# Splitting w_in and w_out once and keeping the parts in DRAM; cache rows moved in 128 and in 16 pieces

## The chip, the core and the metric

The kernel runs on one core of a Trainium2 chip. The metric is the device time of one execution in microseconds (us): the median of three runs. A run is also profiled, and that execution has a time of its own. The core has a matrix engine (TensorE, PE in the profile, with PEld for its weight loads), a vector engine (VectorE, DVE), an activation engine (ScalarE, ACT), a general engine (GpSimd, POOL), and an engine that only issues transfers (SyncE, SP). Each engine works through its own instructions in order, and engines wait for one another and for transfers at semaphores. All transfers of this kernel are issued by SP, one after another.

## The reference, cut to what matters

One layer (DEPTH is 1) works on 2048 prompt rows and 8 sample rows, each of width 1024, all in float32:

```
z = rmsnorm(x) @ w_in                       # 1024 x 1536: q, k, v, conv a and g, ssm u
mix = [attention(q, k, v) | conv(a, g) | ssm(u)]
x = x + mix @ w_out                         # 1024 x 1024
x = x + (silu(hf @ w_gate) * (hf @ w_up)) @ w_down   # hf = rmsnorm(x), 2816 hidden columns
y = rmsnorm(x)
```

Attention has a window of 128 keys. A sample row attends to the 128 rows of its own cache (cache_swa_k and cache_swa_v, each 8 x 128 x 2 x 64). Outputs besides y are the last rows of k, v, conv input and ssm state, and for the samples the caches shifted by one row: rows 1 to 127 of each key and value cache become rows 0 to 126 of the output, and row 127 is the new one. The conv cache (8 x 30 x 256) is shifted in the same way.

## The kernel before

Rows are handled in four quarters of 512 columns (the last has 520, with the 8 samples), transposed so that channels lie on the partitions. A product of float32 matrices is made of three passes of the matrix engine over a high and a low part: weight high by input high, weight high by input low, weight low by input high. So every 128-column block of a weight is first split. `load_unit` does it: SP loads the block (1024 x 128, 512 KB) into a raw tile `wraw` (two buffers), ACT copies it rounded to `whl[:, 0]`, and POOL writes the rest, raw minus rounded, to `whl[:, 1]` (128 x 2 x 1024, 1 MB; three buffers).

Up to the feed-forward part the blocks are used by quarter: twelve blocks of w_in (2 for u, 4 for the conv's g and a, 6 for k, v and q) and then eight of w_out, so each block is loaded and split four times: 48 and 32 units. `w_stream` runs the w_in products; ssm, conv and attention of the quarters run beside it, and their outputs go through DRAM (`mix`). `out_stream` runs the w_out products and `gate_up` and `down` the feed-forward part in two halves, each with its weights loaded anew.

The order of instructions is written by a planner, `Flow`, while the program is built. Tasks say which engine, buffers and events they need next; the planner keeps a clock for each engine, estimates a cost for each instruction (`Engine.cost`), and emits the task that can begin first, with a priority among those close together. The result is a fixed list for each engine, so a changed cost or buffer count moves instructions throughout.

Sample caches are touched at two places. `attn_sample` loads rows 1 to 127 of the key cache into a tile with the row index on the partitions, puts the new row (`nrow`) into the output and into the tile's row 0, and does the same for values. `shift_caches`, at the start of the feed-forward part, copies the shifted rows from the input caches to the outputs inside DRAM.

Of the kernel before, what the change touches and what calls it, by code (L numbers as in the profile page):

```python
# [9 lines left out]
F32 = mybir.dt.float32  # L10
F32R = mybir.dt.float32r
# [150 lines left out]
class Engine:  # L162
# [8 lines left out]
    def cost(self, op, out, ins, args, kw):  # L171
        n = 1
        for d in out.shape[1:]:
            n *= d
        psum = any(x.space == PSUM for x in ins)
        if self.name == "PE":
            if op == "transpose":
                return max(54.0, args[1].shape[0] / 1.2 + 2.5)
            if ins[0].dtype == F32R:
                return max(107.0, n / 2.4 + 2.5)  # L180
            ns = max(215.0, n / 0.6 + 6.0)
            return ns / 2 + 1.0 if out.shape[0] <= 64 else ns
# [29 lines left out]
def hybrid_step(  # L212
# [42 lines left out]
    nsink = const.tile([P, NH], F32, name="nsink")  # L255

    psum = ctx.enter_context(tc.tile_pool(name="psum", bufs=1, space=PSUM))
    wpool = ctx.enter_context(tc.tile_pool(name="wpool", bufs=3))
    hpool = ctx.enter_context(tc.tile_pool(name="hpool", bufs=2))
    stage = ctx.enter_context(tc.tile_pool(name="stage", bufs=1))  # L260
# [5 lines left out]
    spool = segA.enter_context(tc.tile_pool(name="spool", bufs=1))  # L266
    kpool = segA.enter_context(tc.tile_pool(name="kpool", bufs=1))
    N_ST, N_X, N_S2, N_CU = 6, 2, 7, 3
    fl.buffers(mm=3, sc=3, tr=2, wraw=2, whl=3, h=2, stg=N_ST, x=N_X, acc=1, cu=N_CU, s2=N_S2, s4=2, u=2, ssmA=1,
               ssmB=1)  # L270


# [36 lines left out]


    class Unit:
        def __init__(self, load):
            self.load, self.ready, self.hl = load, Ev(), None

    def load_unit(u, prio, pool=None, tag="whl", bufs=3, after=0.0):

        def one():
            yield "SP", "wraw"
            raw = wpool.tile([P, 1024], F32, tag="wraw", name="wraw", bufs=2)
            u.load(raw)  # L320
            yield "ACT", tag
            hl = (pool or wpool).tile([P, 2, 1024], F32R, tag=tag, name=tag, bufs=bufs)
            S.activation(hl[:, 0, :], raw, AF.Copy)
            yield "POOL"
            G.tensor_tensor(hl[:, 1, :], raw, hl[:, 0, :].bitcast(F32), op=OP.subtract)
            rel("wraw")
            u.hl = hl.rearrange("p h (k c) -> p h k c", c=P)
            u.ready.hit(fl.now())
        fl.add(one(), -1e6 + prio, after=after)

    def cols_unit(w, c0s):

        def load(raw):
            r3 = raw.rearrange("p (k c) -> p k c", c=P)
            n = P // len(c0s)
            wv = w.rearrange("(k p) c -> p k c", p=P)
            for i, c0 in enumerate(c0s):
                dma(r3[:, :, i * n:(i + 1) * n], wv[:, :, c0:c0 + n])
        return Unit(load)

    def rows_unit(w, f):
        return Unit(lambda raw: dma(raw, w[f * P:(f + 1) * P, :]))
# [1 line left out]
    def out_unit(m):  # L344


        def load(raw):
            r3 = raw.rearrange("p (k c) -> p k c", c=P)
            cs = slice(m * P, (m + 1) * P)
            for g in range(2):  # L350
                dma(r3[64 * g:64 * g + 64, 0:4, :],
                    w_out[0, 256 * g:256 * g + 256, cs].rearrange("(j p) c -> p j c", p=64))
            dma(r3[:, 4:6, :], w_out[0, 512:768, cs].rearrange("(k p) c -> p k c", p=P))
            for l in range(2):
                dma(r3[:, 6 + l, :], dap(w_out, (768 + 16 * l) * D + m * P, [[32 * D, 8], [D, 16], [1, P]]))
        return Unit(load)

    def product(ps, n, terms, evs=None):

# [99 lines left out]

    def w_units(q, kind):  # L460
        if kind == "u":
            return [("u", i, cols_unit(w_in[0], [1280 + i * P])) for i in range(2)]
        if kind == "c":
            return [(k, i, cols_unit(w_in[0], [b + i * P])) for i in range(2) for k, b in (("g", 1024), ("a", 768))]
        return ([("k", 0, cols_unit(w_in[0], [512])), ("v", 0, cols_unit(w_in[0], [640]))]
                + [("q", j, cols_unit(w_in[0], [64 * j, 256 + 64 * j])) for j in range(4)])

    def w_stream(plan):
        first = []
# [773 lines left out]
    plan = w_plan([(int(x[0]), x[1:]) for x in "0c 0u 1k 0k 1u 1c 2c 2u 3u 2k 3k 3c".split()])  # L1243
    outs = [out_unit(m) for _ in range(4) for m in range(KT)]
    for i, u in enumerate([p[3] for p in plan] + outs):
        load_unit(u, i)
    for q in range(4):
        fl.add(prep_h(q), -2e6 if q == 0 else -1000 + q)
    fl.add(cu_tiles(), -2e6)
# [11 lines left out]
    def s_tile():  # L1261
        return apool.tile([P, 4, 256], F32, tag="s", name="s", bufs=5)
# [175 lines left out]
            mix_ev[q, k].hit(fl.now())  # L1438

    def attn_sample():  # L1440
        yield "SP", kvq_ev[3], dist_ev
        kvT = apool.tile([P, 2, NS], F32, tag="kvT", name="kvT")
        dma(kvT[:, 0, :], kT_d[3][:, 512:520])
        dma(kvT[:, 1, :], vT_d[3][:, 512:520])
# [9 lines left out]
        V.tensor_copy(nrow, pt[:NS, 0:256].rearrange("p (i c) -> p i c", c=P))  # L1454
        rel("tr")
        V.tensor_tensor(qs[:, 0], qs[:, 0], qs[:, 1], op=OP.add)
        yield "SP", "s", "s", "s", "x2"
        kc, vc, kT = [s_tile().rearrange("p j k -> p (j k)").rearrange("p (b c) -> p b c", c=P) for _ in range(3)]
        for i, (t, src, dst) in enumerate(((kc, cache_k, o_ks), (vc, cache_v, o_vs))):
            dma(t[1:P], src[0, :, 1:P].rearrange("b t g d -> t b (g d)"))  # L1460
            dma(dst[0, :, 127].rearrange("b g d -> b (g d)"), nrow[:, i, :])
            dma(t[0:1].rearrange("o b c -> o (b c)").rearrange("o (b c) -> o b c", c=P), nrow[:, i, :])
        for a in range(2):
# [331 lines left out]

    def shift_caches():

        for src, dst in ((cache_k, o_ks), (cache_v, o_vs)):
            yield "SP"
            dma(dst[0, :, 0:127].rearrange("b t g d -> t b (g d)"), src[0, :, 1:128].rearrange("b t g d -> t b (g d)"))  # L1800
        yield "SP"
        dma(o_convs[0, :, 0:29, :].rearrange("b t c -> t b c"), cache_conv[0, :, 1:30, :].rearrange("b t c -> t b c"))

    fl.add(shift_caches(), 300, after=t0)

# [38 lines left out]
    def final(q, i, dst, c0, n):  # L1844
# [26 lines left out]
        if tag == "y":  # L1871
            y = fpool.tile([P, D], F32, tag="y", name="y", bufs=2)
        else:
            y = wpool.tile([P, 2, D], F32R, tag="whl", name="y3").bitcast(F32)[:, 0]
        V.tensor_tensor(st[:n, 0:1], st[:n, 0:1], st[:n, 1:2], op=OP.add)
        yield "ACT"
        S.activation(st[:n, 1:2], st[:n, 0:1], AF.Sqrt, scale=1.0 / D, bias=eps[:n])
# [57 lines left out]
```

## Time and profile before

| | |
|---|---|
| median of three runs | 2398.83 us (2397.98 to 2400.85) |
| the profiled execution | 2399.17 us, span of its instructions 2397.2 us |
| busy: PE, DVE, ACT, POOL | 93%, 49%, 31%, 27% of the span |
| bytes moved | 212.24 MB by the program's queue |

The span is cut below into stretches: 0 to 857 us holds everything ahead of the feed-forward part, 857 to 2397 us the feed-forward part. A row that gives busy time of an engine in a stretch says how much of it the engine worked; the granted clock (PEclk) is 1 for the matrix engine's full speed of 2.4 GHz and 0.5 for 1.2 GHz.

### The profile page before, as it was taken

To read this page: it belongs to the slowest core of one execution; us is meant where nothing else is said; L and a number is where in the kernel's file an instruction comes from. 1 tells how busy PE (TensorE), PEld (TensorE's weight loads), DVE (VectorE), ACT (ScalarE), POOL (GpSimd) and SP (SyncE) were. 2 spreads that over 40 slices of the span, in tenths; PEclk is the share of its full clock that TensorE was granted. 3 is DMA by queue.
4 is the path that set the end of the run, shared out by engine and by line. 5 is a ranking of instruction groups with operands and counts; after the bars stand their busy time and mean duration, and the time that the engine had idled before them with its cause. 6 is when DMAs were issued, how large, how long until landed. Compare 5 with 4: busy or idle time off the path is not lost.

```text
span 2397.2 us, 31412 instructions
## 1 busy us (share of the span) xinstructions
PE 2222.3 (93%) x12518; PEld 1865.2 (78%) x12518; DVE 1163.1 (49%) x2177; ACT 731.6 (31%) x1324; POOL 644.2 (27%) x329
## 2 busy tenths in 40 slices
PE   8878977939899994999999999999999999999998
PEld 8656756737667883888888888888999898989997
DVE  6997979939996551222222222246233332322234
ACT  6227633726665320111111111136111111111113
POOL 3473442212335431221222212221222112222220
PEclk9989988969999997999999999999999999999999
DMA  6444534525646651111111111126111111111101
GB/s 181 114 124 132 132 90 125 152 64 167 181 145 194 195 174 59 53 44 44 53 53 53 40 40 44 53 76 211 53 53 36 45 45 48 45 49 53 53 27 71
DMA packets 301192, 214.24 MB, mean 89 GB/s; under 512 B 61491, under 2 KB 263622, under 8 KB 301046
## 3 DMA queue, kind: packets, MB, share of 16 engines
q1 hardware_dynamic: 301046, 212.24, 30.1%
q8 instruction: 98, 1.61, 0.3%
q14 instruction: 48, 0.39, 0.0%
HBM read 172.39 MB, written 40.48 MB: 89 GB/s over the span
## 4 chain that ended last, share of the span: by engine, by line
PE 74%; DVE 15%; SPq 4%; DMA 2%; POOL 2%; issue 2%; ACT 1%; DVEq 0%; ACTq 0%; POOLq 0%
PE mm L207 47%; PE sc L207 23%; DVE s L207 5%; SPq L149 4%; DVE acc L207 4%; PE tr L207 3%; DVE h L207 1%; POOL s L207 1%; POOL whl L207 1%; DVE stg L207 1%; DVE sst L207 1%; DMA wraw<-in_w_ff_gate 1%; DVE x L207 1%; DVE t L207 1%; DVE ET L207 1%
## 5 line engine op out<-in xcount | busy, mean ns | idle before, releaser
L207 PE MATMUL mm<-h,whl 128*128 128x512 f32 (+2 forms) x7824 | 1508.7, 351 | 24.7 <-DVE stg L207 10.8
L207 PEld LDWEIGHTS mm<-h,whl 128*128 128x128 f32 x7824 | 1256.1, 191 | 234.9 <-issue 12.6
L207 POOL TENSOR_TENSOR whl<-wraw,whl 128x1024 fp32r<-128x1024 f32 x168 | 425.2, 2531 | 1209.3 <-ACT whl L207 1083.1
L207 PE MATMUL sc<-act,whx 128*128 128x512 f32 (+2 forms) x2640 | 507.8, 351 | 29.2 <-ACT act L207 28.9
L207 PEld LDWEIGHTS sc<-act,whx 128*128 128x128 f32 x2640 | 426.9, 189 | 100.2 <-ACT act L207 29.4
L207 DVE TENSOR_TENSOR xa<-xa,sc 128x512 f32<-128x512 f32 (+2 forms) x440 | 255.4, 582 | 340.9 <-PE sc L207 340.8
L207 ACT ACTIVATE whl<-wraw 128x1024 fp32r<-128x1024 f32 x168 | 178.0, 1059 | 640.3 <-PE mm L207 468.5
L207 DVE TENSOR_TENSOR stg<-stg,mm 128x512 f32<-128x512 f32 (+2 forms) x110 | 64.0, 582 | 616.3 <-ACT stg L207 314.5
L207 DVE SCALAR_TENSOR_TENSOR acc<-cu,taps,acc 128x512 f32<-128x512 f32 x240 | 216.6, 964 | 0.0
L207 POOL TENSOR_TENSOR whx<-wraw,whx 128x1024 fp32r<-128x1024 f32 x44 | 105.7, 2402 | 367.1 <-ACT whx L207 352.7
L207 ACT ACTIVATE act<-stg 128x512 fp32r<-128x512 f32 (+2 forms) x110 | 60.2, 548 | 429.5 <-DVE stg L207 429.5
L207 DVE TENSOR_TENSOR act<-stg,act 128x512 fp32r<-128x512 f32 (+2 forms) x110 | 96.6, 878 | 66.7 <-ACT act L207 66.7
L207 ACT ACTIVATE whx<-wraw 128x1024 fp32r<-128x1024 f32 x44 | 46.3, 1052 | 220.2 <-PE sc L207 220.2
L207 ACT ACTIVATE stg<-mm 128x512 f32<-128x512 f32 (+2 forms) x144 | 75.1, 522 | 84.0 <-PE mm L207 83.9
L207 ACT ACTIVATE s<-s,sst 128x256 f32<-128x256 f32 (+1 forms) x184 | 85.2, 487 | 15.7 <-DVE sst L207 15.6
L207 ACT ACT_TABLE_LOAD x59 | 75.7, 1283 | 4.0 <-DMA out<-s 1.7
L207 POOL TENSOR_TENSOR stg<-stg 128x512 f32<-128x512 f32 (+2 forms) x33 | 46.0, 1394 | 41.8 <-ACT stg L207 34.3
L207 PE MATMUL sc<-kk,qq 128*128 128x256 f32 (+1 forms) x304 | 44.8, 292 | 10.3 <-DVE mx L207 9.1
L207 PE MATMUL sc<-ident,s 128*128 128x128 f32 x248 | 39.6, 284 | 14.2 <-DVE s L207 10.9
L207 PEld LDWEIGHTS sc<-kk,qq 128*128 128x128 f32 x304 | 39.4, 195 | 13.9 <-DVE mx L207 7.9
L207 PEld LDWEIGHTS sc<-ident,s 128*128 128x128 f32 x248 | 29.1, 142 | 25.5 <-DVE s L207 14.7
L207 DVE CUSTOM_DVE_ANT_0 s<-sc,ndist 128x256 f32<-128x256 f32 (+1 forms) x128 | 45.6, 408 | 2.7 <-PE sc L207 2.6
(201 smaller groups left out, 1206.1 us busy)
## 6 DMA issues: line engine op xcount, KB each, us to landing
wraw<-in_w_ff_gate SPq DMA_DIRECT2D x44, 512.0 KB
wraw<-in_w_ff_up SPq DMA_DIRECT2D x44, 512.0 KB
wraw<-in_w_ff_down SPq DMA_DIRECT2D x44, 512.0 KB
wraw<-in_w_in SPq DMA_DIRECT2D x32, 512.0 KB
wraw<-in_w_out SPq DMA_DIRECT2D x96, 128.0 KB
wraw<-in_w_in SPq DMA_DIRECT2D x32, 256.0 KB
mix<-stg SPq DMA_DIRECT2D x32, 256.0 KB
xo<-in_x_prompt SPq DMA_DIRECT2D x32, 256.0 KB
```

The lines of the kernel that those rows point to most:

```text
L149: r = self.nc.sync.dma_start(out, in_)
L207: return call(*args, **kw)
```

## The change

Four things change in the program.

1. Each block of w_in and w_out is split at its first use only. Its whole `whl` tile (both parts, 1 MB) is then stored to a DRAM tile `kept`; each of the three later uses loads that tile straight into a `whl` buffer, with no `wraw`, ACT or POOL. Of the 80 units 20 are split and stored and 60 are reloaded. A chain of events (`turn`) keeps the units' buffers in order.
2. `whl` has four buffers in place of three.
3. `attn_sample` loads all 128 rows of each sample cache, ahead of its other loads, and `shift_caches` copies each shifted cache as 16 pieces for each of the 8 samples (1016 or 464 elements each) in place of 127 (or 29) rows for each sample.
4. The planner's cost of a matmul of split operands is n / 2.4 + 18 ns for n columns (before + 2.5), and 123 ns at least (before 107).

```diff
             if ins[0].dtype == F32R:
-                return max(107.0, n / 2.4 + 2.5)
+                return max(123.0, n / 2.4 + 18.0)
...
-    fl.buffers(mm=3, sc=3, tr=2, wraw=2, whl=3, h=2, stg=N_ST, x=N_X, acc=1, cu=N_CU, s2=N_S2, s4=2, u=2, ssmA=1,
+    fl.buffers(mm=3, sc=3, tr=2, wraw=2, whl=WB, h=2, stg=N_ST, x=N_X, acc=1, cu=N_CU, s2=N_S2, s4=2, u=2, ssmA=1,
...
+        mine, taken = turn.get(tag), Ev()
+        turn[tag] = taken
+        order = (mine,) if mine else ()
+
+        def again():
+            yield "SP", tag, kept_ev[u.key], *order
+            taken.hit(0.0)
+            hl = (pool or wpool).tile([P, 2, 1024], F32R, tag=tag, name=tag, bufs=bufs)
+            dma(hl.bitcast(F32), kept[u.key])
+            u.hl = hl.rearrange("p h (k c) -> p h k c", c=P)
+            u.ready.hit(fl.now())
 
         def one():
             yield "SP", "wraw"
             raw = wpool.tile([P, 1024], F32, tag="wraw", name="wraw", bufs=2)
             u.load(raw)
-            yield "ACT", tag
+            yield "ACT", tag, *order
+            taken.hit(0.0)
...
             u.ready.hit(fl.now())
+            if keep:
+                yield "SP"
+                dma(kept[u.key], hl.bitcast(F32))
+                kept_ev[u.key].hit(fl.now())
+        if u.key is not None and u.key in kept:
+            fl.add(again(), -1e6 + prio, after=after)
+            return
+        if keep:
+            kept[u.key] = dram.tile([P, 2, 1024], F32, name="hl_%s%d" % u.key)
+            kept_ev[u.key] = Ev()
         fl.add(one(), -1e6 + prio, after=after)
...
     for i, u in enumerate([p[3] for p in plan] + outs):
-        load_unit(u, i)
+        load_unit(u, i, keep=True)
...
     def attn_sample():
-        yield "SP", kvq_ev[3], dist_ev
+        yield "SP", kvq_ev[3], dist_ev, "s", "s", "s", "x2"
+        kc, vc, kT = [s_tile().rearrange("p j k -> p (j k)").rearrange("p (b c) -> p b c", c=P) for _ in range(3)]
+        for t, src in ((kc, cache_k), (vc, cache_v)):
+            dma(t, src[0].rearrange("b t g d -> t b (g d)"))
...
-        yield "SP", "s", "s", "s", "x2"
-        kc, vc, kT = [s_tile().rearrange("p j k -> p (j k)").rearrange("p (b c) -> p b c", c=P) for _ in range(3)]
-        for i, (t, src, dst) in enumerate(((kc, cache_k, o_ks), (vc, cache_v, o_vs))):
-            dma(t[1:P], src[0, :, 1:P].rearrange("b t g d -> t b (g d)"))
+        yield "SP"
+        for i, (t, dst) in enumerate(((kc, o_ks), (vc, o_vs))):
             dma(dst[0, :, 127].rearrange("b g d -> b (g d)"), nrow[:, i, :])
...
-        for src, dst in ((cache_k, o_ks), (cache_v, o_vs)):
+        for src, dst, row, rows in ((cache_k, o_ks, 128, 128), (cache_v, o_vs, 128, 128), (cache_conv, o_convs, 256, 30)):
             yield "SP"
-            dma(dst[0, :, 0:127].rearrange("b t g d -> t b (g d)"), src[0, :, 1:128].rearrange("b t g d -> t b (g d)"))
-        yield "SP"
-        dma(o_convs[0, :, 0:29, :].rearrange("b t c -> t b c"), cache_conv[0, :, 1:30, :].rearrange("b t c -> t b c"))
+            n = (rows - 1) * row // 16
+            dims = [[n, 16], [rows * row, NS], [1, n]]
+            dma(dap(dst, 0, dims), dap(src, row, dims))
```

SP's list where the sample caches are loaded, before (a row is one instruction, with its line, what it writes and reads, the shape, and a count where it stands several times; `mr` are loads for the next quarter's `out_stream` input, `stg<-vT` the values of a quarter for attention):

```order
L149 DMA mr<-mix_78 128x512 x2
L149 DMA wraw<-in_w_out 64x4x128 x2
L149 DMA wraw<-in_w_out 128x2x128
L149 DMA wraw<-in_w_out 128x1x128 x2
L149 DMA s<-in_cache_swa_k 127x8x128
L149 DMA out<-nrow 8x128
L149 DMA s<-nrow 1x8x128
L149 DMA s<-in_cache_swa_v 127x8x128
L149 DMA out<-nrow 8x128
L149 DMA s<-nrow 1x8x128
L149 DMA mr<-mix_78 128x512
L149 DMA stg<-vT_76 128x512
```

The same place in the changed kernel (`kvT` and `qs` are the sample's own rows, `hl_o` the kept blocks of w_out, `x_82` stores of the first quarter's rows, `xo` loads of x):

```order
L149 DMA wraw<-in_w_ff_gate 128x8x128
L149 DMA s<-in_cache_swa_k 128x8x128
L149 DMA s<-in_cache_swa_v 128x8x128
L149 DMA kvT<-kT_73 128x8
L149 DMA kvT<-vT_77 128x8
L149 DMA qs<-qh_65 128x4x8
L149 DMA qs<-ql_69 128x4x8
L149 DMA x_82<-x_5855 128x512
L149 DMA xo<-in_x_prompt 128x4x128
L149 DMA hl_o_200<-whl 128x2048
L149 DMA wraw<-in_w_ff_up 128x8x128
L149 DMA whl<-hl_o_193 128x2048
```

The two cache loads now stand together with 128 rows each, the stores of the new row come later, and the whole place has moved behind the loads of all eight blocks of w_out (before, behind two); stores of kept blocks and their first reloads stand around it.

SP's list at the start of the feed-forward part, before (`wraw` are its weights, `xa` the rows it adds to, `rs` the row norms):

```order
L149 DMA xa<-x_83 128x512 x5
L149 DMA rs_89<-stg 128x520
L149 DMA out<-in_cache_swa_k 127x8x128
L149 DMA wraw<-in_w_ff_gate 128x8x128
L149 DMA wraw<-in_w_ff_up 128x8x128
L149 DMA out<-in_cache_swa_v 127x8x128
L149 DMA out<-in_cache_conv 29x8x256
L149 DMA wraw<-in_w_ff_gate 128x8x128
L149 DMA wraw<-in_w_ff_up 128x8x128
```

The same place in the changed kernel:

```order
L149 DMA wraw<-in_w_ff_gate 128x8x128
L149 DMA xa<-x_83 128x512 x3
L149 DMA wraw<-in_w_ff_up 128x8x128
L149 DMA xa<-x_83 128x512 x2
L149 DMA out<-in_cache_swa_k 16x8x1016
L149 DMA wraw<-in_w_ff_gate 128x8x128
L149 DMA out<-in_cache_swa_v 16x8x1016
L149 DMA wraw<-in_w_ff_up 128x8x128
L149 DMA out<-in_cache_conv 16x8x464
```

The three copies still stand among the weight loads, in 16 outer pieces now, with one weight load between two of them.

POOL's list from the ssm of the second quarter on (`stg<-s,s` is the last product of a quarter's ssm, two for each quarter, `stg<-acc` and the products behind it the conv's norm), before:

```order
L207 TENSOR_TENSOR stg<-s_2595,s_2372 128x512
L207 TENSOR_TENSOR stg<-s_2614,s_2372 128x512
L207 TENSOR_TENSOR whl<-wraw,whl 128x1024 x5
L207 TENSOR_TENSOR stg<-acc 128x512
L207 TENSOR_TENSOR stg<-stg 128x512
L207 TENSOR_TENSOR whl<-wraw,whl 128x1024
L207 TENSOR_TENSOR stg<-s_3122,s_3039 128x512
L207 TENSOR_TENSOR stg<-s_3142,s_3039 128x512
L207 TENSOR_TENSOR stg<-stg,acc 128x512 x2
L207 TENSOR_TENSOR whl<-wraw,whl 128x1024 x3
L207 TENSOR_TENSOR stg<-s_3486,s_3364 128x512
L207 TENSOR_TENSOR stg<-s_3500,s_3364 128x512
```

And in the changed kernel:

```order
L207 TENSOR_TENSOR stg<-s_2481,s_2286 128x512
L207 TENSOR_TENSOR stg<-s_2494,s_2286 128x512
L207 TENSOR_TENSOR stg<-acc 128x512
L207 TENSOR_TENSOR stg<-stg 128x512
L207 TENSOR_TENSOR stg<-stg,acc 128x512 x2
L207 TENSOR_TENSOR stg<-s_3101,s_3029 128x512
L207 TENSOR_TENSOR stg<-s_3123,s_3029 128x512
L207 TENSOR_TENSOR stg<-s_3424,s_3342 128x512
L207 TENSOR_TENSOR stg<-s_3433,s_3342 128x512
L207 TENSOR_TENSOR stg<-acc 128x512
L207 TENSOR_TENSOR stg<-stg 128x512
L207 TENSOR_TENSOR stg<-stg,acc 128x512 x2
```

The splits `whl<-wraw,whl` no longer stand between the ssm and conv work of the second to the last quarter; the next ones are the eight blocks of w_out.

## Rows read from the trace of the kernel before

**Rows 1.** The page's second part: PE's busy tenths in 40 equal slices.

```profile
PE   8878977939899994999999999999999999999998
```

**Rows 2.** Busy time by stretch: engines, instructions, granted clock, DMA share, GB/s.

```profile
core 0: us, PE busy (x) PEld busy (x) DVE busy (x) ACT busy (x) POOL busy (x), PEclk, DMA share, GB/s
0.00:110.00 110.00, 93.17 (x562) 82.78 (x562) 88.89 (x241) 50.65 (x81) 43.71 (x39) 0.92 0.57 149
110.00:484.00 374.00, 318.05 (x2162) 246.82 (x2162) 331.32 (x599) 190.14 (x342) 155.21 (x88) 0.91 0.46 126
484.00:532.00 48.00, 10.60 (x74) 10.01 (x74) 7.17 (x12) 5.78 (x8) 5.04 (x3) 0.64 0.11 35
532.00:650.00 118.00, 108.15 (x591) 84.23 (x591) 112.14 (x305) 77.47 (x208) 35.89 (x21) 0.94 0.61 171
650.00:857.00 207.00, 195.52 (x1107) 158.98 (x1108) 142.67 (x256) 105.55 (x217) 93.63 (x50) 0.97 0.60 176
960.00:2397.00 1437.00, 1426.60 (x7744) 1227.12 (x7742) 449.39 (x733) 285.85 (x449) 295.87 (x123) 1.00 0.18 56
```

**Rows 3.** Who PE waited for, 480 to 600 and 800 to 960 us: total, times, longest.

```profile
PE tr L207 <- DMA stg<-vT: 21.7, 1, 21.7
PE tr L207 <- DMA s<-nrow: 16.2, 1, 16.2
...
PE sc L207 <- ACT act L207: 28.9, 1, 28.9
```

**Rows 4.** SP's instructions in order of time at the sample caches: start, length.

```profile
481.04 0.44 SPq L149 DMA_DIRECT2D s<-in_cache_swa_k  x1
481.57 22.26 SPq L149 DMA_DIRECT2D out<-nrow  x1
...
505.11 22.81 SPq L149 DMA_DIRECT2D out<-nrow  x1
```

**Rows 5.** SP's instructions in order of time at the shifted copies.

```profile
876.16 25.66 SPq L149 DMA_DIRECT2D wraw<-in_w_ff_gate  x1
...
904.91 24.07 SPq L149 DMA_DIRECT2D out<-in_cache_conv  x1
929.10 7.32 SPq L149 DMA_DIRECT2D wraw<-in_w_ff_gate  x1
```

**Rows 6.** Busy time by stretch, right behind the two stops at the caches.

```profile
507.00:511.00 4.00, 3.26 (x14) 2.89 (x14) 0.69 (x1) 0.00 (x0) 0.00 (x0) 0.50 0.07 22
532.00:538.00 6.00, 5.52 (x26) 5.55 (x27) 5.27 (x24) 5.26 (x13) 2.56 (x2) 0.50 0.94 235
```

**Rows 7.** Groups by line and shape, 0 to 860 us: busy, mean | idle before, releaser.

```profile
L207 DVE SCALAR_TENSOR_TENSOR acc<-cu,taps,acc 128x512 f32<-128x512 f32 x240 | 216.6, 964 | 0.0
L207 DVE TENSOR_SCALAR s<-s,sst 128x256 f32<-128x256 f32 x72 | 37.0, 576 | 0.5
...
L207 POOL TENSOR_TENSOR whl<-wraw,whl 128x1024 fp32r<-128x1024 f32 x83 | 220.1, 2653 | 409.0 <-ACT whl L207 282.8 <-issue 58.2 <-DMA qq<-qh 14.0
...
L207 ACT ACTIVATE whl<-wraw 128x1024 fp32r<-128x1024 f32 x83 | 87.8, 1058 | 189.8 <-PE mm L207 112.6 <-DMA wraw<-in_w_in 51.8 <-issue 20.4
```

**Rows 8.** Single tiles' instructions: duration in ns, minimum, median, maximum, first and last start.

```profile
L207 DVE SCALAR_TENSOR_TENSOR acc<-cu,taps,acc x240: 721/744/2905, 49.5 to 705.4; 128x512 f32<-128x512 f32 x120
...
L207 DVE TENSOR_SCALAR s<-s,sst x72: 340/349/2504, 435.1 to 729.5; 128x256 f32<-128x256 f32 x72
```

**Rows 9.** Instructions in order of time near 422 us: start, length.

```profile
421.81 2.35 POOL L207 TENSOR_TENSOR whl<-wraw,whl 128x1024 fp32r<-128x1024 f32 x1 [16.28 <-ACT whl L207]
421.85 2.33 DVE L207 TENSOR_TENSOR sst<-sst,nsink 128x4 f32<-128x4 f32 x1
```

**Rows 10.** The chain that ended last, 110 to 484 us, by engine and line.

```profile
by line: DVE acc L207 18.9%; PE mm L207 18.5%; DVE s L207 16.3%; PE sc L207 14.5%; PE tr L207 6.3%; POOL whl L207 5.3%; POOL s L207 5.0%; issue 4.1%; DVE stg L207 3.2%; DVE tmp_s L207 1.6%; DVE h L207 1.4%; DVE x L207 1.0%; DVE sst L207 0.9
```

**Rows 11.** Busy time by stretch of the instructions that touch whl alone.

```profile
110.00:484.00 374.00, 208.41 (x1016) 164.71 (x1016) 34.95 (x33) 100.35 (x34) 0.91 0.46 126
```

**Rows 12.** Busy time by stretch, where transfers were densest.

```profile
860.00:880.00 20.00, 20.00 (x87) 16.15 (x87) 15.84 (x14) 8.97 (x13) 7.06 (x3) 1.00 0.98 350
```

More of the change, by code (lines that the diff above doesn't have):

```diff
@@ L257, in hybrid_step @@
     psum = ctx.enter_context(tc.tile_pool(name="psum", bufs=1, space=PSUM))
+    WB = 4
     wpool = ctx.enter_context(tc.tile_pool(name="wpool", bufs=3))
@@ L311, in hybrid_step, with __init__, load_unit @@
     class Unit:
-        def __init__(self, load):
-            self.load, self.ready, self.hl = load, Ev(), None
-    def load_unit(u, prio, pool=None, tag="whl", bufs=3, after=0.0):
+        def __init__(self, load, key=None):
+            self.load, self.ready, self.hl, self.key = load, Ev(), None, key
+    kept, kept_ev, turn = {}, {}, {}
+    def load_unit(u, prio, pool=None, tag="whl", bufs=WB, after=0.0, keep=False):
+        mine, taken = turn.get(tag), Ev()
[8 more added lines that the diff above has]
+            u.ready.hit(fl.now())
         def one():
@@ L328, in one, with cols_unit @@
             u.ready.hit(fl.now())
+            if keep:
[8 more added lines that the diff above has]
+            kept_ev[u.key] = Ev()
         fl.add(one(), -1e6 + prio, after=after)
-    def cols_unit(w, c0s):
+    def cols_unit(w, c0s, key=None):
         def load(raw):
@@ L338, in load @@
                 dma(r3[:, :, i * n:(i + 1) * n], wv[:, :, c0:c0 + n])
-        return Unit(load)
+        return Unit(load, key)
     def rows_unit(w, f):
@@ L355, in load @@
                 dma(r3[:, 6 + l, :], dap(w_out, (768 + 16 * l) * D + m * P, [[32 * D, 8], [D, 16], [1, P]]))
-        return Unit(load)
+        return Unit(load, ("o", m))
     def product(ps, n, terms, evs=None):
@@ L461, in w_units @@
         if kind == "u":
-            return [("u", i, cols_unit(w_in[0], [1280 + i * P])) for i in range(2)]
+            return [("u", i, cols_unit(w_in[0], [1280 + i * P], ("u", i))) for i in range(2)]
         if kind == "c":
-            return [(k, i, cols_unit(w_in[0], [b + i * P])) for i in range(2) for k, b in (("g", 1024), ("a", 768))]
-        return ([("k", 0, cols_unit(w_in[0], [512])), ("v", 0, cols_unit(w_in[0], [640]))]
-                + [("q", j, cols_unit(w_in[0], [64 * j, 256 + 64 * j])) for j in range(4)])
+            return [(k, i, cols_unit(w_in[0], [b + i * P], (k, i))) for i in range(2)
+                    for k, b in (("g", 1024), ("a", 768))]
+        return ([("k", 0, cols_unit(w_in[0], [512], ("k", 0))), ("v", 0, cols_unit(w_in[0], [640], ("v", 0)))]
+                + [("q", j, cols_unit(w_in[0], [64 * j, 256 + 64 * j], ("q", j))) for j in range(4)])
     def w_stream(plan):
@@ L1873, in final @@
         else:
-            y = wpool.tile([P, 2, D], F32R, tag="whl", name="y3").bitcast(F32)[:, 0]
+            y = wpool.tile([P, 2, D], F32R, tag="whl", name="y3", bufs=WB).bitcast(F32)[:, 0]
         V.tensor_tensor(st[:n, 0:1], st[:n, 0:1], st[:n, 1:2], op=OP.add)
```

## The prediction

> **What bounds the kernel now.** I read the page's slices first: PE is busy all the time in the last six tenths and has gaps in the first four [rows 1]. The table by stretch says the same in us [rows 2]: from 960 us on PE works 1426.6 of 1437 us at full clock, so nothing that frees another engine or a buffer can be felt there. Ahead of 857 us it works 93.2, 318.1, 10.6, 108.2 and 195.5 us in five stretches, 725 of 857: 132 us stand idle. In the second stretch DVE is the busier engine (331 of 374 us). The third, 484 to 532 us, is different in kind: PE, DVE, ACT and POOL all rest, and the transfers too (share 0.11, against 0.46 and 0.61 on either side).
>
> The waits name who ended the rests: 16.2 and 21.7 us until transfers, and 28.9 us at the start of the feed-forward part behind ACT [rows 3], at a time when the weight loads were held on SP [rows 5]. SP's own rows show why. The load of the key cache is issued in 0.44 us, and then SP's next instruction, a store of 4 KB, is held 22.26 us; behind the value cache the same, 22.81 us [rows 4]. That load is 127 rows x 8 x 512 bytes = 520 KB; over 22.3 us this is 23 GB/s, one sixteenth of the 350 GB/s that all engines reach in the densest stretch [rows 12]. So one transfer engine of 16 carries the whole load, and SP, which works in order, stands behind it with every other transfer. The shifted copies do it again: the weight load behind the first copy is held 25.66 us, the conv copy behind the second 24.07, the next weight load 7.32 [rows 5]. Two places, then, and beside them a DVE bound up to 484 us.
>
> **The change part by part. Cache rows in 128 and 16 pieces.** Rows that divide by 16 should use all engines: 0.52 MB at 350 GB/s is 1.5 us, the two loads and three copies together some 7 us of transfer beside 421 us that are free ahead of 857 us (worked out below). Removed are the rests: 16.2 + 21.7 + 28.9 = 66.8 us. The matmuls right behind the first two ran at a granted clock of 0.5 (1.2 GHz): 3.26 and 5.52 us of work [rows 6], half of it lost time, 4.4 us. **Term 1: -71.2 us.** What is late next? In the stop DVE did 7.2 of 48 us and ACT 5.8 [rows 2], so no engine caught up on work that it would now owe; I keep the whole term. Its other end is nothing, if the new shapes stay on one engine (rival D).
>
> **Splits removed.** Sixty of 80 units lose an ACT copy (1.06 us) and a POOL subtraction (2.65 us) [rows 7]. Neither engine is a bound, but POOL's split stretches DVE's work: at 421.81 us POOL begins a split of 2.35 us, and a DVE operation on four columns that begins 0.04 us later takes 2.33 us and ends with it [rows 9]. How much that is in all I take from mean against median: the conv's 240 multiply-adds have a mean of 964 and a median of 744 ns, 52.8 us over; the softmax's 72 scalings 576 and 349, 16.3 us [rows 7, 8]. Of these 69 us, 60 of 83 splits should give back 50. (Smaller groups would add, other POOL work takes away; I let them cancel.) Only what lies on the path counts: in 110 to 484 us the chain gives DVE 18.9 + 16.3 + 3.2 + 1.6 + 1.4 + 1.0 + 0.9 = 43.3% [rows 10], 162 of its 331 busy us, so 0.49 of it: 24.5 us. The chain also has POOL's splits at 5.3%, 20 us; 34 splits stand in this stretch [rows 11], the last of the first twelve blocks among them, which remain, so I take half, 10. **Term 2: -34.5 us.** Ends: nothing, if PE takes over as the bound at once; and 77 us, all the rest that PE has in 110 to 484, 532 to 650 and 650 to 857 us (55.9 + 9.9 + 11.5).
>
> The Trainium skill has a rule that makes more of it (page "SBUF — State Buffer", section "Who interferes with whom"): a DVE instruction with two SBUF inputs and a GpSimd instruction that reads SBUF exclude each other, and the second to issue waits for the whole of the first. The trace agrees in kind [rows 9]; by the rule at its fullest the 60 splits would hold DVE for their whole length, and the sum would be that of rival B below.
>
> **Stores and reloads.** A kept unit moves 1.05 MB, 3.0 us of all engines at 350 GB/s [rows 12]. A raw block is 0.52 MB; in the feed-forward part, where little but such blocks moves, 56 GB/s take a share of 0.18, so 311 GB/s when full, 1.7 us [rows 2]. Before: 80 x 1.7 = 136 us. After: 20 x (1.7 + 3.0) + 60 x 3.0 = 274. So 138 us more. Free ahead of 857 us, by the shares of its five stretches [rows 2]: 47 + 202 + 43 + 46 + 83 = 421 us. It fits on average. It is tight at the start: twelve stores, 36 us, into 47 free. I let a quarter of that delay first loads. **Term 3: +8 us** (ends 0 and 138).
>
> SP's queue: a store waits for its POOL split, and behind it stands the raw load after next, which waited for the same split before, since that frees its `wraw`: no cost. A reload waits on SP for PE to let go of a buffer; ACT had that wait before, 112.6 us of it [rows 7]. Behind it on SP stand stores of k, q, u and mix, and reads of the next stage. With four buffers three blocks are ahead; 24 matmuls at 208.4 us / 1016 [rows 11] are 4.9 us, so 15 us of cover for a transfer of 3. I cost it at nothing; with the cover gone it is rival C. Where w_out took five issues a block, it takes one now: SP gains, and nobody waits for that.
>
> **Planner numbers and the fourth buffer.** PE's and DVE's work is the same but for a few copies that change places with ACT. The feed-forward part has PE full, so the deeper buffer gives nothing there. The new order can shift waits either way; I cost it at 0 with 10 us on both sides, half of the 21 us for which PE rests in 532 to 857 us.
>
> **Sum.** -71.2 - 34.5 + 8 = -97.7 us on the profiled execution's 2399.2 (span 2397.2 and 2.0 around it): 2301.5. The median of the runs is 0.3 below the profiled one: 2301 us.
>
> **Rivals.**
> A, only the stops go: DVE's stretched operations lie where PE is the bound anyway. For it: PE has 318 of 374 us of work in the DVE stretch, and its work at half clock is not won back by anything. Against: the chain's 43% DVE. 2399.2 - 71.2 + 8 = 2336 us.
> B, every removed split frees DVE for its whole length: 60 x 2.65 x 0.49 = 78 us on the path, capped by PE's 77 us of rest. For it: single operations do stretch by a whole split [rows 9]. Against: half of the operations keep their median [rows 8], so most meet no split. 2399.2 - 71.2 - 77 + 8 = 2259 us. (This is what the page on SBUF would make of it at its fullest.)
> C, slower: the reloads are not hidden, the 138 us of transfers stand on the path of the w_in and w_out products. For it: shares of 0.6 from 532 us on, and SP in order. Against: 421 us free and 15 us of cover. 2399.2 - 71.2 - 34.5 + 138 = 2431 us; it turns slower once more than 106 of the 138 us are felt, 1.8 us for each reload.
> D, the change doesn't do what it says: the new shapes still run on one engine, and the stops stay. 2399.2 - 34.5 + 8 = 2373 us. For it: nothing but that the 8 samples lie inside. By the Trainium skill (page "DMA: Bandwidth & Descriptors", section on why a DMA increments its semaphore by 16) the count of engines is the largest number up to 16 that divides the outermost size, so 1 for 127 and 16 for 128 or 16; the trace agrees for 127 [rows 4].
>
> **How the numbers follow.** Chances: the forecast 0.54 (its own range 2280 to 2322, by the planner's 10 us and about a third of term 2), A 0.24, B 0.13, C 0.05, D 0.04. The range from 2258 to 2340 takes in the forecast, nearly all of A and over half of B, and leaves out C, D and the far side of B. What a measurement can tell is 0.2%, 5 us. A, B, D and the forecast are all faster, C is slower but for a sliver: faster 0.94, same 0.01, slower 0.05.
>
> **What would show it.** Term 1: no SP instruction of 20 us at the caches, no PE wait over 10 us there or at the start of the feed-forward part, and no stretch with every engine at rest. Term 2: a mean of the conv's multiply-adds near 800 ns, fewer than 30 splits ahead of the feed-forward part, DVE's share of the chain there smaller than PE's. Term 3: a share of transfers near 0.7 with reloads landing before PE asks; waits of PE for reloads, or waits of SP for PE that hold mix or u stores, would be C. The feed-forward part should take as long as before less 29 us. Most likely to make me wrong is the size of term 2: it rests on a chain's share, and which engine bounds the first half once the splits are gone is not in this trace.

## The result, and the profile of the changed kernel

The changed kernel takes 2319.07 us in the median (2313.35 to 2322.32), beside 2399.72 for the kernel before, run with it: a ratio of 0.9662, 95% interval 0.9640 to 0.9684, or 80.7 us less. The forecast was 2301 with a range of 2258 to 2340. The profiled execution took 2316.92 us.

The page's first two parts, busy time of the engines and PE's slices (against [rows 1]):

```profile
PE 2213.1 (96%) x12518; PEld 1860.5 (80%) x12518; DVE 1074.2 (46%) x2187; ACT 674.2 (29%) x1261; POOL 473.3 (20%) x263
...
PE   8689989999699999999999999999999999999997
```

The slices of 3 and 4 at the two stops are gone. What stands below 8 now is a 6 in the second slice, a 6 in the eleventh, from 579 us on, and a 7 at the end. DVE is busy for 1074.2 us (before 1163.1), POOL for 473.3 (before 644.2).

Busy time by stretch (columns as in [rows 2]; here the feed-forward part begins at some 806 us):

```profile
0.00:110.00 110.00, 86.86 (x535) 77.26 (x536) 82.74 (x255) 49.23 (x79) 44.39 (x49) 0.91 0.86 263
110.00:484.00 374.00, 340.64 (x2316) 264.79 (x2315) 312.64 (x723) 189.42 (x418) 44.25 (x37) 0.94 0.61 188
484.00:650.00 166.00, 142.26 (x800) 110.42 (x800) 113.59 (x330) 82.78 (x213) 32.77 (x20) 0.92 0.71 215
650.00:810.00 160.00, 152.05 (x866) 129.06 (x865) 91.24 (x120) 51.92 (x87) 44.44 (x29) 0.99 0.74 252
...
880.00:2315.00 1435.00, 1421.27 (x7709) 1222.70 (x7707) 444.49 (x730) 284.80 (x446) 287.88 (x120) 1.00 0.18 55
```

The stretch to 110 us has PE less busy than before (86.9 us against 93.2) with transfers at a share of 0.86, where it was 0.57. From 110 to 484 us PE works 340.6 us (318.1 before). The feed-forward part is full, as it was.

Who PE waited for, 0 to 880 us (total, times, longest; against [rows 3]):

```profile
PE mm L207 <- POOL whl L207: 14.7, 2, 13.6
PE tr L207 <- POOL s L207: 12.9, 1, 12.9
PE sc L207 <- DVE s L207: 12.3, 13, 2.8
PE tr L207 <- POOL stg L207: 11.1, 4, 5.2
...
PE tr L207 <- DMA stg<-in_cache_conv: 5.1, 1, 5.1
PE tr L207 <- ACT ss L207: 4.2, 1, 4.2
```

No wait of 16 to 29 us is left, and none for the key and value caches; one of 5.1 us is for the samples' conv cache. Two of 13 us remain. In the first, at some 83 us, among the stores of the first twelve blocks, PE waits for a split, and POOL's rows show what held it (start, length, and in brackets the idle time before and what ended it):

```profile
91.22 2.46 POOL L207 TENSOR_TENSOR s<-s,PW 128x128 f32<-128x128 f32 x3 [16.94 <-DVE s L207]
93.64 2.78 POOL L207 TENSOR_TENSOR whl<-wraw,whl 128x1024 fp32r<-128x1024 f32 x1
```

ACT had rounded the block by 87.4 us. In POOL's order the split stands behind a product of the ssm's set-up, for which POOL waited 16.9 us until DVE was done.

SP's instructions at the sample caches and at the shifted copies, in order of time (start, length; against [rows 4, 5]):

```profile
580.84 0.79 SPq L149 DMA_DIRECT2D s<-in_cache_swa_k  x1
581.73 2.94 SPq L149 DMA_DIRECT2D s<-in_cache_swa_v  x1
...
592.05 0.99 SPq L149 DMA_DIRECT2D out<-nrow  x1
...
832.81 0.69 SPq L149 DMA_DIRECT2D out<-in_cache_swa_k  x1
836.97 0.39 SPq L149 DMA_DIRECT2D wraw<-in_w_ff_gate  x1
837.40 0.63 SPq L149 DMA_DIRECT2D out<-in_cache_swa_v  x1
```

Nothing on SP is held for 20 us any more: 2.94 us is the longest of these rows.

The groups that the second term spoke of, whole span and, for the splits, 0 to 800 us (busy, mean; against [rows 7]):

```profile
L207 DVE SCALAR_TENSOR_TENSOR acc<-cu,taps,acc 128x512 f32<-128x512 f32 x240 | 174.5, 791 | 0.1
...
L207 DVE TENSOR_SCALAR s<-s,sst 128x256 f32<-128x256 f32 x76 | 27.4, 424 | 0.6
...
L207 POOL TENSOR_TENSOR whl<-wraw,whl 128x1024 fp32r<-128x1024 f32 x24 | 58.7, 2450 | 206.3 <-ACT whl L207 175.4 <-DMA xo<-in_x_prompt 20.2 <-DMA wraw<-in_w_out 9.0
```

The conv's multiply-adds fell from a mean of 964 to 791 ns, 42 us in all; their median stayed at 743. There are 24 splits ahead of the feed-forward part where there were 83.

The chain that ended last, 110 to 484 us (against [rows 10]):

```profile
by line: PE mm L207 30.1%; PE sc L207 17.1%; PE tr L207 10.8%; DVE s L207 10.7%; DVE acc L207 8.5%; POOL s L207 3.3%; ACT s L207 2.8%; issue 2.8%; ACT stg L207 2.3%; SPq L149 2.0%; DVE stg L207 1.9%; ACT L207 1.9%; DVE TT L207 1.1%; DVE h L
```

The conv's share fell from 18.9 to 8.5%, and that of DVE's `s` tiles (most of them the ssm's here, the rest the softmax's) from 16.3 to 10.7; PE's matmuls now lead.

By the start of its k-th instruction (PE executes 12518 in every version) the changed kernel gains at the two old stops and gives some back between. This table is worked out from the start times in the traces, changed less before, us:

```
k        1000    2500    3000    3500    4700    5000   12000   12500
time    -6      -17.8   -57.6   -74.6   -51     -88     -87.2   -80.7
```

The first stop falls between 2500 and 3000 (-39.8), the second between 4700 and 5000 (-37). What the kept blocks gain up to 3500 is partly lost again by 4700, and 6.5 us more go in the last products.

### The profile page after: what moved, and what is told of

Same layout as the page of the kernel before. It is cut to its first block, busy times and chain, and to the rows that moved or that the text cites. A ratio compares the mean times of both kernels' runs of the same rounds, so it can differ in the third digit from the quotient of the medians.

```text
span 2315.1 us, 31098 instructions
## 1 busy us (share of the span) xinstructions
PE 2213.1 (96%) x12518; PEld 1860.5 (80%) x12518; DVE 1074.2 (46%) x2187; ACT 674.2 (29%) x1261; POOL 473.3 (20%) x263
## 3 DMA queue, kind: packets, MB, share of 16 engines
q1 hardware_dynamic: 234745, 264.67, 36.2%
## 4 chain that ended last, share of the span: by engine, by line
PE 82%; DVE 10%; ACT 2%; DMA 2%; issue 2%; POOL 1%; SPq 1%; DVEq 0%; ACTq 0%; POOLq 0%
PE mm L207 54%; PE sc L207 25%; PE tr L207 4%; DVE s L207 4%; DVE acc L207 2%; SPq L149 1%; DVE h L207 1%; DMA x<-in_x_prompt 1%; DVE stg L207 1%; ACT s L207 1%; POOL s L207 1%; ACT L207 1%; ACT stg L207 0%; DVE ET L207 0%; DVE x L207 0%
## 5 line engine op out<-in xcount | busy, mean ns | idle before, releaser
L207 POOL TENSOR_TENSOR whl<-wraw,whl 128x1024 fp32r<-128x1024 f32 x108 | 261.0, 2418 | 1087.1 <-ACT whl L207 1045.9
L207 ACT ACTIVATE whl<-wraw 128x1024 fp32r<-128x1024 f32 x108 | 114.3, 1060 | 468.7 <-PE mm L207 432.1
L207 DVE SCALAR_TENSOR_TENSOR acc<-cu,taps,acc 128x512 f32<-128x512 f32 x240 | 174.5, 791 | 0.1
```

What stands on the lines that cost most here:

```text
L207: return call(*args, **kw)
```

## The experiments

The theory after the result: the stops gave what the first term said; the kept blocks gave at least what the second said; and something that had been costed at nothing took a part back. Suspects: the planner's new cost, the 138 us of transfers, the fourth buffer, or that splits were never worth so much (rival A).

### The cache shapes alone

The kernel before, with both edits to the cache transfers and nothing else.

```diff
-            dma(t[1:P], src[0, :, 1:P].rearrange("b t g d -> t b (g d)"))
+            dma(t, src[0].rearrange("b t g d -> t b (g d)"))
...
-            dma(dst[0, :, 0:127].rearrange("b t g d -> t b (g d)"), src[0, :, 1:128].rearrange("b t g d -> t b (g d)"))
+            n = (rows - 1) * row // 16
+            dims = [[n, 16], [rows * row, NS], [1, n]]
+            dma(dap(dst, 0, dims), dap(src, row, dims))
```

> The kernel before, in its own order, with only the cache shapes changed: sample caches loaded in 128 rows, shifted copies in 16 pieces. Theory (the stops are one transfer engine carrying a whole load): both stops go, 71 to 77 us less, so 2323 to 2329 us, no SP instruction over 10 us at the caches. Rival (the stops come from something else near them, or move to the next wait): less than 30 us gained, above 2370 us.

Measured: 2321.46 us (2319.88 to 2322.50), ratio 0.9668 (0.9654 to 0.9681): 79.8 us less. SP at the caches, where the two `out<-nrow` had been held over 22 us each:

```profile
482.47 0.45 SPq L149 DMA_DIRECT2D s<-in_cache_swa_k  x1
483.02 0.43 SPq L149 DMA_DIRECT2D out<-nrow  x1
...
487.23 0.39 SPq L149 DMA_DIRECT2D s<-in_cache_swa_v  x1
487.67 0.47 SPq L149 DMA_DIRECT2D out<-nrow  x1
```

By PE's instructions the first stop gave 39.6 us and the second 37.4; nothing else moved. These few lines alone give the time of the whole change (2319). So the rest of the change, 60 splits fewer included, came to nothing in sum, and the question is what cancelled them.

### The old cost of a matmul

The changed kernel with one line as it was.

```diff
-                return max(123.0, n / 2.4 + 18.0)
+                return max(107.0, n / 2.4 + 2.5)
```

> The changed kernel with the planner's old matmul cost (107 and 2.5 ns) throughout. Theory (the new cost moved the samples' attention and conv behind the prompt's attention, where PE waits for it, about 25 us, and a worse order of the last products, about 6): their loads stand beside the prompt's attention again, 2283 to 2295 us. Rival (the order hardly matters, the rest of the gain was never there): within 6 us of the changed kernel, 2313 to 2325.

Measured: 2269.76 us (2266.47 to 2272.72), ratio 0.9453 (0.9437 to 0.9469), 49 us better than the changed kernel, and more than expected. The table by stretch:

```profile
110.00:484.00 374.00, 350.43 (x2443) 277.19 (x2444) 314.37 (x703) 191.92 (x387) 51.43 (x42) 0.97 0.68 215
484.00:650.00 166.00, 160.40 (x859) 120.91 (x856) 146.34 (x387) 105.89 (x286) 34.39 (x25) 1.00 0.76 233
650.00:810.00 160.00, 155.88 (x877) 134.17 (x876) 74.53 (x93) 45.42 (x74) 43.28 (x24) 0.99 0.74 248
```

PE works 350.4 of 374 us and 160.4 of 166, against 340.6 and 142.3 in the changed kernel. The sample caches are loaded at 424 us instead of 581. By the start of its k-th instruction PE is ahead of the changed kernel by 10 us at the 1000th, 25 at the 2500th, 18 at the 3500th and 44 at the 4000th: over half of it goes between the last two, from 601 to 732 us in the changed kernel, where its late samples stand.

### The old cost only ahead of the feed-forward part

```diff
+                return max(123.0, n / 2.4 + 18.0) if Engine.LATE else max(107.0, n / 2.4 + 2.5)
...
     t0 = segB_ev.t
+    Engine.LATE = True
```

> The changed kernel with the old matmul cost ahead of the feed-forward part and the new one in it. Theory: about 25 us less than the changed kernel, 2290 to 2298, and about 6 us more than with the old cost throughout. Rival (the end is the same under both costs): the same time as with the old cost throughout.

Measured: 2272.95 us (2272.43 to 2273.88), ratio 0.9467 (0.9454 to 0.9480). So 46 of the 49 us lie ahead of the feed-forward part, and some 3 in the order of the last products (6 in the profiled executions).

### No block kept, under either cost

The changed kernel with `load_unit(u, i)` for `load_unit(u, i, keep=True)`: every block split at each use, no stores and no reloads. First with the new cost:

> The changed kernel with every use of w_in and w_out split anew (nothing kept, nothing reloaded), all else as changed. Theory (POOL's splits stretch DVE, 34.5 us on the path less 8 for transfers): 15 to 35 us slower than the changed kernel, 2334 to 2354 us, the conv's mean multiply-add back above 920 ns. Rival (keeping gives nothing): within 6 us of the changed kernel.

Measured: 2354.65 us (2346.11 to 2359.41), ratio 0.9802 (0.9780 to 0.9823). Then with the old cost:

> The changed kernel with the old matmul cost and every block split anew at each use (no stores, no reloads); all else as changed. It stands to the 2269.8 us of the old cost with kept blocks as the run without keeping stood to the changed kernel, there 35 us. If keeping is worth about 50 us in this order, as the forecast's terms and the cache shapes alone (2321 us) let one expect, 2312 to 2325 us with a mean multiply-add of the conv over 900 ns; if the fourth buffer gave a part of it, 2295 to 2311.

Measured: 2330.19 us (2328.78 to 2332.86), ratio 0.9711 (0.9698 to 0.9725). So keeping blocks is worth 36 us under the new cost and 60 under the old. The last is more than expected. The conv's group and the splits of the run with the old cost:

```profile
L207 DVE SCALAR_TENSOR_TENSOR acc<-cu,taps,acc 128x512 f32<-128x512 f32 x240 | 210.1, 934 | 0.0
...
L207 POOL TENSOR_TENSOR whl<-wraw,whl 128x1024 fp32r<-128x1024 f32 x168 | 429.9, 2559 | 1210.8 <-ACT whl L207 1121.0 <-issue 21.3 <-DMA qq<-ql 15.9
```

Its chain from 110 to 484 us:

```profile
by line: DVE acc L207 24.3%; DVE s L207 17.5%; PE sc L207 12.7%; PE mm L207 11.0%; issue 4.6%; POOL whl L207 4.4%; PE tr L207 4.3%; DVE stg L207 3.1%; SPq L149 3.0%; DMA wraw<-in_w_in 2.3%; DVE h L207 1.9%; DVE sst L207 1.9%; DVE x L207 1.6
```

Without keeping, DVE's conv and `s` tiles hold 41.8% of the chain there; with it, same cost, they hold 7.9:

```profile
by line: PE mm L207 39.9%; PE sc L207 11.2%; PE tr L207 8.4%; issue 8.1%; SPq L149 4.4%; DVE acc L207 4.1%; DVE s L207 3.8%; DMA ql<-stg 3.3%; ACT s L207 3.0%; DMA mr<-mix 2.6%; POOL s L207 2.4%; DMA out<-s 1.8%; DVE stg L207 1.7%; DMA stg<
```

DVE's busy time over the whole span is 1153.9 us without and 1072.4 with kept blocks: 81.5 us freed by 60 splits, and 60 us of it felt.

### Three buffers

The old cost, kept blocks, and `WB = 3`.

> The changed kernel with the planner's old matmul cost and three whl buffers in place of four. With four it took 2269.8 us. If a reload of 3.0 us has cover enough in three buffers (two blocks ahead, some 10 us of matmuls), 2270 to 2280 us; if the fourth buffer is what hides the reloads, 2290 to 2320, with more waits of PE for reloads of whl and the conv's mean multiply-add still near 790 ns.

Measured: 2283.97 us (2282.64 to 2285.50), ratio 0.9516 (0.9503 to 0.9529): between the two, 14 us for the fourth buffer. PE waited once, 2.2 us, for a reload and 25.7 us in three waits for splits (13.9 in one with four buffers), so the reloads were hidden by three buffers too. With no block kept no gain shows: 2330 with four beside 2321 with three (the cache shapes alone, where `attn_sample` also loads in its old place).

### POOL's work, put back

Is it POOL's work that DVE feels? The changed kernel, in its own order, with 60 more subtractions on constant data.

```diff
             dma(hl.bitcast(F32), kept[u.key])
+            wide = ones32.unsqueeze(1).to_broadcast([P, 2, 512])
+            nc.gpsimd.tensor_tensor(scr.rearrange("p (h c) -> p h c", h=2), wide, wide, op=OP.subtract)
```

> The changed kernel with 60 more subtractions of 128 x 1024 on POOL, one behind each reload's place in the program, on constant data: POOL waits for nothing there and holds no buffer. The output is the same. If POOL's work itself takes time by stretching DVE's, as my second term has it, the conv's mean multiply-add rises from 791 to 880 ns or more and the time from 2319 to 2339 to 2385 us (the 64 us by which the same work on the reloaded tile exceeded its small control are the upper end). If the 64 us came only from POOL holding back buffers, the mean may rise but the time stays under 2327.

Measured: 2373.16 us (2371.66 to 2374.95), ratio 0.9889 (0.9876 to 0.9903): 54 us more. The conv's group and the added one:

```profile
L207 DVE SCALAR_TENSOR_TENSOR acc<-cu,taps,acc 128x512 f32<-128x512 f32 x240 | 210.0, 938 | 0.1
...
L336 POOL TENSOR_TENSOR scr<-ones 128x1024 bf16<-128x1024 f32 x60 | 129.8, 2163 | 1.9
```

The mean rose from 791 to 938 ns. The chain from 110 to 484 us:

```profile
by line: DVE acc L207 26.7%; DVE s L207 17.7%; PE mm L207 17.1%; PE sc L207 11.9%; PE tr L207 6.0%; DVE stg L207 4.3%; issue 3.8%; DMA whl<-hl_g 2.2%; DVE h L207 1.7%; DVE x L207 1.4%; ACT stg L207 1.2%; DVE sst L207 1.2%; DVE TT L207 1.1%;
```

Who PE waited for, 0 to 880 us:

```profile
PE sc L207 <- DVE s L207: 28.0, 13, 6.0
PE mm L207 <- POOL whl L207: 18.3, 2, 13.7
PE tr L207 <- DVE h L207: 15.0, 6, 7.5
PE tr L207 <- POOL stg L207: 14.8, 5, 7.4
PE tr L207 <- POOL s L207: 11.3, 1, 11.3
```

No one waits for the added work itself, and what stands behind it in POOL's queue is little later: PE's waits for POOL are 44.4 us in these three rows, 38.7 in the same rows of the changed kernel. Those for DVE's `s` tiles went from 12.3 to 28.0, most of the rise before products of the ssm, and in the chain DVE's conv and `s` tiles hold 44.4% where they held 19.2. So it is DVE. 129.8 us of POOL's work cost 54 us, 0.42 for each us. The 60 splits removed, 170 us of POOL (429.9 us for 168, 259.7 for the 108 that remain), gave 60, or 0.35 for each.

Two runs of the first attempt at this read the reloaded tile, so that POOL also waited for each reload and the buffer was held; one with the whole tile and one, a control, with 8 columns:

```diff
             dma(hl.bitcast(F32), kept[u.key])
+            nc.gpsimd.tensor_tensor(scr, hl[:, 0, :].bitcast(F32), hl[:, 1, :].bitcast(F32), op=OP.subtract)
```

> The changed kernel in its own order, with one POOL subtraction of a split's size added behind each of the 60 reloads, on the reloaded tile, its result not used. Theory (what keeping the parts gives is POOL out of DVE's way): most of the gain of keeping is lost again, 20 to 36 us slower than the changed kernel, 2339 to 2355, the conv's mean multiply-add from 791 to over 900 ns. Rival (the gain is ACT's time, or shorter waits for a ready block): within 8 us of the changed kernel, though the mean rises.

> The control to the run with added POOL work: the same 60 subtractions at the same places with the same waits, on 8 columns in place of 1024. Theory: within 6 us of the changed kernel, the conv's mean near 791 ns. Rival (it is POOL's waits for the reloads that cost, not the length of its work): as slow as with 1024 columns.

Measured: 2421.01 us (2419.95 to 2422.82), ratio 1.0095 (1.0081 to 1.0109), and 2357.16 (2351.95 to 2358.98), ratio 0.9825 (0.9810 to 0.9839). Both missed: the control alone costs 38 us. Its POOL row:

```profile
L333 POOL TENSOR_TENSOR scr<-whl 128x8 bf16<-128x8 f32 x60 | 47.5, 792 | 447.9 <-DMA whl<-hl_o 134.9 <-DMA whl<-hl_q 107.8 <-DMA whl<-hl_a 86.7
```

POOL, in order, stood 447.9 us ahead of these, mostly for reloads, with the ssm's and the conv's products queued behind it (PE's waits for POOL's `stg` rose from 11.1 to 34.6 us), while the conv's mean was 773 ns. That is a cost of a wait put into an engine's queue and of a buffer held for it, which these runs do not tell apart, and nothing of it is in the change. The 64 us between the two go with the length of POOL's work and are of the size of the 54 of the cleaner run; the longer operation also holds its buffer longer, so they are not shown to be DVE's alone.

### More transfers

The changed kernel, each reload followed by a copy of the same 1 MB inside DRAM, for which nobody waits.

```diff
             dma(hl.bitcast(F32), kept[u.key])
+            nc.sync.dma_start(dram.tile([P, 2, 1024], F32, name="more%d" % len(more)), kept[u.key])
```

> The changed kernel in its own order, with one copy of each kept block inside DRAM (1 MB, to a place never read) behind each of the 60 reloads: by 3.0 us for 1.05 MB some 180 us more of transfers ahead of the feed-forward part. Theory (transfers are mostly hidden; 138 us more cost about 8): 5 to 30 us slower, 2324 to 2349. Rival (transfers are felt one for one): 120 us slower or more, above 2440.

Measured: 2377.93 us (2373.47 to 2380.20), ratio 0.9912 (0.9898 to 0.9926): 59 us more, a miss. By stretch:

```profile
110.00:484.00 374.00, 317.52 (x2121) 243.17 (x2119) 289.15 (x636) 168.50 (x344) 44.57 (x39) 0.94 0.79 275
484.00:650.00 166.00, 146.40 (x901) 116.81 (x900) 101.84 (x360) 91.72 (x262) 26.80 (x15) 0.95 0.77 241
650.00:810.00 160.00, 129.60 (x568) 102.16 (x568) 97.23 (x142) 48.30 (x82) 32.02 (x23) 0.88 0.88 328
```

At shares of 0.79, 0.77 and 0.88, where the changed kernel had 0.61, 0.71 and 0.74, a third of the added 180 us (60 x 3.0) is felt. By the profiler's count of packet time the added copies took less, 144 us (41.3% of 2378.4 us against 36.2% of 2315.1), and the change's own added transfers 117 us (30.1% of 2397.2 us before) and not 138; by that count 0.41 is felt. A part of it shows as loads that land later (PE's waits, 0 to 880 us; the changed kernel has none of this name):

```profile
PE tr L207 <- DMA xo<-in_x_prompt: 22.0, 12, 4.3
```

"It fits on average" does not make a transfer free. The run adds its transfers on top of a share that the change had already raised, so at the same rate the change's own would cost 45 to 48 us, which is likelier too much than too little; the run does not measure it.

### A tile of its own for the samples' attention

Under the new cost `attn_sample` stands late, since its `Z` takes an `x2` buffer that the w_out residuals also use. Late means alone, as the stretches of the changed kernel show:

```profile
601.00:613.00 12.00, 6.91 (x58) 6.41 (x57) 10.66 (x40) 4.50 (x9) 1.46 (x2) 0.99 0.89 330
613.00:634.00 21.00, 8.51 (x29) 6.10 (x30) 19.62 (x38) 7.03 (x14) 3.23 (x3) 0.50 0.30 90
```

PE works 15 of 33 us there, the last 21 at half clock. The edit gives `Z` a buffer of its own; the second run does it under the old cost.

```diff
-        yield "SP", kvq_ev[3], dist_ev, "s", "s", "s", "x2"
+        yield "SP", kvq_ev[3], dist_ev, "s", "s", "s"
...
-        Z = opool.tile([P, NS, 64], F32, tag="x2", name="Z", bufs=2)
+        Z = opool.tile([P, NS, 64], F32, tag="Z", name="Z", bufs=1)
```

> The changed kernel, new matmul cost and all, but the samples' attention has a tile of its own for Z in place of one of the two x2 buffers, for which the residuals of the w_out products stand in line with it. Theory (with the new cost those residuals take x2 first, so the samples' attention is put off until the prompt's is over, and PE waits through its chain): its loads move ahead by 61 rows of SP's list, and 15 to 25 us are won, 2294 to 2304 us. Rival (the late samples are a bystander, the new cost harms elsewhere): within 6 us of the changed kernel.

> The changed kernel with the old matmul cost, and the sample attention's Z in a tile of its own. If the samples were late only by the new cost's order, nothing changes: 2266 to 2274 us. If they also wait for x2 in the old order, 2252 to 2265.

Measured: 2307.13 us (2301.28 to 2311.07), ratio 0.9617 (0.9601 to 0.9634), under the new cost, with the key cache loaded at 488 us instead of 581: 12 us better (4 to 17 by the two intervals) but less than expected; 2266.44 (2264.05 to 2269.87), ratio 0.9445 (0.9433 to 0.9458), under the old, which the intervals do not tell from 2269.76. So the place of the samples' attention is about a quarter of what the new cost took, between a tenth and somewhat over a third. The samples' conv did not move: its cache is still loaded at 610 us (461 under the old cost), and PE still waits there, 5.7 us for that load and 7.9 us for a product of POOL's behind it. The old cost with kept blocks, with or without this edit, is the fastest version, some 5.5% below the kernel before.

## Why the prediction came out as it did

Four runs form a chain from the kernel before to the changed one. By differences of their ratios times 2399.7 us: the cache shapes -80 (0.9668); the fourth buffer and the earlier place of the cache loads in `attn_sample`, with no block kept, +10 (0.9711); kept blocks under the old cost -62 (0.9453); the new cost +50 (0.9662).

**Term 1, the stops: right.** Forecast -71.2, measured -80 alone. The first stop gave 39.6, against 37.9 + 4.4 by the forecast; the second 37.4 against 28.9, since the wait that was read, 28.9 us, is the longest one and not all that the held weight loads cost. Two more waits of PE for weight blocks there took 1.9 and 1.7 us, and the kernel before ran its next products at a lowered clock:

```profile
900.00:930.00 30.00, 14.16 (x52) 10.40 (x50) 0.00 (x0) 2.11 (x2) 4.68 (x2) 0.79 0.19 54
930.00:965.00 35.00, 18.00 (x68) 14.18 (x69) 7.20 (x10) 3.71 (x5) 4.75 (x2) 0.69 0.21 64
```

Their 120 matmuls took 32.2 us; at the 232 ns that one takes at full clock (below) they would take 27.8, 4.3 less. Together that is 36.8 us. Every sign named for it came: no SP instruction of 20 us, no PE wait over 10 us there, no stretch at rest. SP's store behind the key cache's load takes 0.43 us with 128 rows, where it took 22.26 with 127. The Trainium skill's rule on the outermost size (page "DMA: Bandwidth & Descriptors", section "Why a DMA increments its semaphore by 16 and not by 1") gives 16 engines for 128 and one for 127, and the trace agrees. Rival D is out.

**Term 2, the splits: right in kind, too small.** The three signs came: 791 ns, 24 splits, DVE's share of the chain below PE's. With term 3 it was to be worth -26.5 net; it was -60 under the old cost and -36 under the new. The forecast looked at two groups of DVE (50 us given back) and let the rest cancel; DVE as a whole got 81.5 us back, and 0.74 of it was felt under the old cost rather than the chain's 0.49, net of whatever the stores and reloads cost. Rival A is out by the run that put POOL's work back. Rival B, DVE freed for the splits' whole length, is out as a mechanism, since 81.5 us were freed for 170 us of POOL; its price, 77 us, was nearer than the forecast's 34.5. The Trainium skill (page "SBUF — State Buffer", section "Who interferes with whom") has the second instruction wait for the whole of the first; the trace shows that for single ones [rows 9], and over all splits half of it.

**Term 3, +8 for transfers: not settled.** (A quarter of the 36 us that it names is 9.) Its signs came: shares of 0.61 to 0.74 behind 110 us, and no wait of PE for a reload. Put on top, 180 us of transfers cost 59, so a price of 8 for 138 us is likely too low, and rival C's one for one is out. The start, of which the term spoke, shows no lasting cost. In the stretch to 110 us, with the share at 0.86, PE waits 13.6 us for a split, but about half of that is POOL's order, and the runs without stores wait near the same place for DVE, 9.5 us under the old cost and 5.3 under the new. At PE's 1000th instruction the changed kernel and the run that keeps no block under the same cost are both 5.9 us ahead of the kernel before. One comparison points to a cost later on. The run with POOL's work put back keeps its blocks and took 2373 us; splitting every block anew took 2355, with POOL busy for longer (652.2 us against 603.6). So stores and reloads may cost some 20 us. The two also differ in the planner's order, and the price by itself was not isolated.

**The failed step: "Planner numbers and the fourth buffer ... I cost it at 0 with 10 us on both sides."** The fourth buffer does give 14 us with kept blocks, but the planner's new cost took 49, and so the kernel ended 18 us above the forecast and not some 30 below it. What that cost took hangs on the rest of the order: 49 us with kept blocks, 41 when `Z` has its own buffer, 24 with no block kept. The bound of 10 was half of PE's rest from 532 to 857 us in the old order; it said nothing of what a new order can lose elsewhere. That the total still came near is luck in part: the stops gave 9 us more than forecast and the kept blocks 35 more, and 60 us that stood at nothing (50 for the new cost, 10 for the fourth buffer with the earlier cache loads) took that back and 16 more. And the new number is the truer one. The table by stretch of the changed kernel, in the feed-forward part:

```profile
1000.00:1200.00 200.00, 200.00 (x862) 1.00 0.16 48
```

862 matmuls of 512 columns in 200 us are 232 ns each; the new cost says 231, the old 216. The planner picks greedily what can begin first, and with the truer number it put the samples' attention behind the residuals and more of DVE's `s` tiles on the path (10.7% of the chain from 110 to 484 us, against 3.8% with the old cost). About a quarter of the 46 us ahead of the feed-forward part is shown to be the samples' attention. The samples' conv, late in both runs with the new cost, is a suspect that no run tests; which other moves in the order make the rest stays open.

## What to carry to other kernels

A number in a planner or a scheduler is a change of the whole order: cost it with a range as wide as the waits it could create, or run it alone; a truer cost need not give a better order. What a stop costs is what every instruction behind it starts later, which can exceed the longest wait in the list. Work taken from POOL paid through DVE here, by the whole of DVE's busy time and not by the two groups in which it is easiest to see.

## What was unexpected in the hardware

POOL's length counts though no one waits for it: 129.8 us of subtractions on constant data raised DVE's busy time from 1074.2 to 1134.5 us and the time by 54. Copies between DRAM tiles for which no engine waits cost 59 us for an estimated 180 us of transfers, with the share still under 0.9. A small POOL operation behind each of 60 reloads, 8 columns wide, cost 38 us by the waits that it brought, with DVE no busier (1065.6 us).
